# A 4096x4096x4096 matrix product with leaky ReLU: regions that fill PSUM, A transposed once by VectorE in 32x32 blocks with a permuted k, B streamed, order fixed by hand

## The chip, the core and the metric

One core of a Trainium2 chip. The metric is the device time of one launch in microseconds (us). The executions of the kernel before agree within about 0.3%. The profile is one execution, its span 1 to 2 us below the timed one.

## The reference

```python
# a: 4096 x 4096, b: 4096 x 4096, float32; alpha = 0.01
x = np.matmul(a, b)
return np.where(x > 0, x, alpha * x)
```

## The kernel before

It multiplies in bf16. For each of four blocks of 1024 columns it loads B as 32 tiles of 128x1024 and casts them into one cache; then it goes through the 32 row tiles of A. In the first block A is cast, stored as bf16 in DRAM, and transposed by TensorE; in the other three it comes back through a transposing DMA.

```python
b_3d = b.rearrange("(ko ki) n -> ki ko n", ki=P)
...
b_cache_pool = ctx.enter_context(tc.tile_pool(name="b_cache", bufs=1))
b_load_pool = ctx.enter_context(tc.tile_pool(name="b_load", bufs=3))
...
for nb in range(N_BLOCKS):
    b_cache = b_cache_pool.tile([P, K_TILES, N_BLOCK], BF16)
    for ko in range(K_TILES):
        b_ld = b_load_pool.tile([P, N_BLOCK], FP32)
        nc.sync.dma_start(b_ld, b_3d[:, ko, nb * N_BLOCK:(nb + 1) * N_BLOCK])
        nc.any.tensor_copy(b_cache[:, ko, :], b_ld)
    for mo in range(M_TILES):
        aT = at_pool.tile([P, K_TILES, P], BF16)
        if nb == 0:
            # ... load t_in, cast to t_bf, store t_bf to DRAM ...
            for ko in range(K_TILES):
                tp = at_psum_pool.tile([P, P], BF16)
                nc.tensor.transpose(tp, t_bf[:, ko * P:(ko + 1) * P], ident)
                nc.vector.tensor_copy(aT[:, ko, :], tp)
        else:
            nc.sync.dma_start_transpose(aT, a_bf_dram[mo][:])
        for nt in range(NT_PER_BLOCK):
            # ... 32 matmuls 128x512 into one PSUM bank, Lrelu on ScalarE, store ...
```

Of the kernel before, what the change touches and what calls it, by code (L numbers as in the profile page):

```python
# [1 line left out]

# [5 lines left out]


@with_exitstack
def kernel(
    ctx: ExitStack,
    tc: tile.TileContext,
    a: bass.AP,
    b: bass.AP,
    alpha,
    out: bass.AP,
):
    nc = tc.nc  # L20
    P = 128
    M, K = a.shape
    K2, N = b.shape
    assert K == K2
    BF16 = mybir.dt.bfloat16
    FP32 = mybir.dt.float32

    M_TILES = M // P
    K_TILES = K // P
    N_TILE = 512  # L30
    N_BLOCK = 1024
    N_BLOCKS = N // N_BLOCK
    NT_PER_BLOCK = N_BLOCK // N_TILE

    alpha = float(alpha)

    a_3d = a.rearrange("(mo mi) k -> mi mo k", mi=P)
    b_3d = b.rearrange("(ko ki) n -> ki ko n", ki=P)
    out_3d = out.rearrange("(mo mi) n -> mi mo n", mi=P)

    dram_pool = ctx.enter_context(tc.tile_pool(name="dram", bufs=M_TILES, space=bass.MemoryType.DRAM))
    a_bf_dram = [dram_pool.tile([P, K], BF16, name=f"a_bf_{i}") for i in range(M_TILES)]

    ident_pool = ctx.enter_context(tc.tile_pool(name="ident", bufs=1))
    ident = ident_pool.tile([P, P], BF16)
    make_identity(nc, ident)

    a_ld_pool = ctx.enter_context(tc.tile_pool(name="a_ld", bufs=2))
    a_bf_pool = ctx.enter_context(tc.tile_pool(name="a_bfp", bufs=2))
    at_pool = ctx.enter_context(tc.tile_pool(name="at", bufs=3))  # L50
    at_psum_pool = ctx.enter_context(tc.tile_pool(name="at_psum", bufs=2, space=bass.MemoryType.PSUM))

    b_cache_pool = ctx.enter_context(tc.tile_pool(name="b_cache", bufs=1))
    b_load_pool = ctx.enter_context(tc.tile_pool(name="b_load", bufs=3))

    psum_pool = ctx.enter_context(tc.tile_pool(name="psum", bufs=4, space=bass.MemoryType.PSUM))
    o_pool = ctx.enter_context(tc.tile_pool(name="oo", bufs=4))

    for nb in range(N_BLOCKS):
        b_cache = b_cache_pool.tile([P, K_TILES, N_BLOCK], BF16)  # L60
        for ko in range(K_TILES):
            b_ld = b_load_pool.tile([P, N_BLOCK], FP32)
            nc.sync.dma_start(b_ld, b_3d[:, ko, nb * N_BLOCK:(nb + 1) * N_BLOCK])  # L63
            nc.any.tensor_copy(b_cache[:, ko, :], b_ld)  # L64

        for mo in range(M_TILES):
            aT = at_pool.tile([P, K_TILES, P], BF16)
            if nb == 0:
                t_in = a_ld_pool.tile([P, K], FP32)
                nc.sync.dma_start(t_in, a_3d[:, mo, :])  # L70
                t_bf = a_bf_pool.tile([P, K], BF16)
                nc.any.tensor_copy(t_bf, t_in)  # L72
                nc.sync.dma_start(a_bf_dram[mo][:], t_bf)  # L73
                for ko in range(K_TILES):
                    tp = at_psum_pool.tile([P, P], BF16)
                    nc.tensor.transpose(tp, t_bf[:, ko * P:(ko + 1) * P], ident)  # L76
                    nc.vector.tensor_copy(aT[:, ko, :], tp)  # L77
            else:
                nc.sync.dma_start_transpose(aT, a_bf_dram[mo][:])  # L79

            for nt in range(NT_PER_BLOCK):
                psum = psum_pool.tile([P, N_TILE], FP32)
                for ko in range(K_TILES):
                    nc.tensor.matmul(  # L84
                        psum,
                        aT[:, ko, :],
                        b_cache[:, ko, nt * N_TILE:(nt + 1) * N_TILE],
                        start=(ko == 0),
                        stop=(ko == K_TILES - 1),
                    )  # L90
                o_sb = o_pool.tile([P, N_TILE], FP32)
                nc.scalar.activation(  # L92
                    o_sb, psum, mybir.ActivationFunctionType.Lrelu, alpha=alpha
                )
                nc.sync.dma_start(  # L95
                    out_3d[:, mo, nb * N_BLOCK + nt * N_TILE: nb * N_BLOCK + (nt + 1) * N_TILE],
                    o_sb,
                )


# [1 line left out]
_INS = ['a', 'b', 'alpha']  # L102
_OUTS = [((4096, 4096), 'float32')]
#: Inputs that are plain numbers.
_NUMBERS = {'alpha': 0.009999999776482582}


# [26 lines left out]
```

## Time and profile before

| | |
|---|---|
| time | 2023.7 us (2021.2 to 2024.8) |
| matmul pace in quiet stretches | 215.8 ns |
| bytes moved, mean rate | 337 MB, 167 GB/s |
| granted TensorE clock, mean | 0.974 |

In a line of the groups, the part after the first bar is the busy time and the mean of one instruction, and the part after the second is how long the engine sat idle just before such instructions, with what ended the wait. In a table of stretches the last three numbers are the granted clock, the mean busy share of the 16 DMA engines and GB/s. The prediction below shows the lines and reads them.

### The profile page before, as it was taken

To read this page: it belongs to the slowest core of one execution; us is meant where nothing else is said; L and a number is where in the kernel's file an instruction comes from. 1 tells how busy PE (TensorE), PEld (TensorE's weight loads), DVE (VectorE), ACT (ScalarE), POOL (GpSimd) and SP (SyncE) were. 2 spreads that over 40 slices of the span, in tenths; PEclk is the share of its full clock that TensorE was granted. 3 is DMA by queue.
4 is the path that set the end of the run, shared out by engine and by line. 5 is a ranking of instruction groups with operands and counts; after the bars stand their busy time and mean duration, and the time that the engine had idled before them with its cause. 6 is when DMAs were issued, how large, how long until landed. Compare 5 with 4: busy or idle time off the path is not lost.

```text
span 2022.0 us, 21113 instructions
## 1 busy us (share of the span) xinstructions
PE 1870.9 (93%) x9032; PEld 865.5 (43%) x9216; DVE 232.5 (11%) x1033; ACT 390.8 (19%) x409; POOL 0.7 (0%) x6
## 2 busy tenths in 40 slices
PE   4699999999977999999995999999997799999999
PEld 1244445555432444444442344444443244444444
DVE  1244444444410000000000000000000000000000
ACT  5423222222224000000015100000002400000000
POOL 0000000000000000000000000000000000000000
PEclk8799999999999999999998999999998999999999
DMA  8975666665379554554558754554556855554552
GB/s 302 344 289 219 229 233 237 237 231 219 141 214 264 125 112 107 125 105 114 125 108 280 194 120 101 123 109 111 124 117 185 246 126 106 116 121 107 116 120 63
DMA packets 460894, 336.95 MB, mean 167 GB/s; under 512 B 403456, under 2 KB 403456, under 8 KB 452608
## 3 DMA queue, kind: packets, MB, share of 16 engines
q1 hardware_dynamic: 460800, 335.59, 60.2%
q8 instruction: 72, 1.18, 0.2%
q14 instruction: 22, 0.18, 0.0%
HBM read 134.22 MB, written 100.66 MB: 116 GB/s over the span
## 4 chain that ended last, share of the span: by engine, by line
PE 85%; DMA 10%; ACT 2%; SPq 1%; DVE 1%; issue 1%; ACTq 0%
PE psum L84 82%; DMA b_ld<-in_b_dram 9%; PE tp L76 3%; ACT b_cache L64 2%; DVE aT L77 1%; SPq L79 1%; DMA t_in<-in_a_dram 1%; ACT t_bf L72 0%; SPq L63 0%; SPq L95 0%; DVE b_cache L64 0%; SPq L73 0%; ACT o_sb L92 0%; ACTq L92 0%
## 5 line engine op out<-in xcount | busy, mean ns | idle before, releaser
L84 PE MATMUL psum<-b_cache,aT 128*128 128x512 bf16 x8008 | 1859.0, 383 | 111.1 <-ACT b_cache L64 100.4
L84 PEld LDWEIGHTS <-aT 128*128 128x128 bf16 x8192 | 804.2, 99 | 1115.4 <-issue 179.6
L92 ACT ACTIVATE o_sb<-psum 128x512 f32<-128x512 f32 x256 | 151.6, 596 | 1274.0 <-PE psum L84 1121.9
L77 DVE COPY aT<-tp 128x128 bf16<-128x128 bf16 x1024 | 226.5, 224 | 327.0 <-PE tp L76 284.6
L76 PE MATMUL tp<-ident,t_bf 128*128 128x128 bf16 x1024 | 219.3, 221 | 36.4 <-ACT t_bf L72 25.7
L72 ACT CAST t_bf<-t_in 128x4096 bf16<-128x4096 f32 x32 | 115.4, 3606 | 231.3 <-PE tp L76 220.0
L64 ACT CAST b_cache<-b_ld 128x1024 bf16<-128x1024 f32 x119 | 124.3, 1044 | 122.4 <-DMA b_ld<-in_b_dram 122.4
L64 DVE CAST b_cache<-b_ld 128x1024 bf16<-128x1024 f32 x9 | 6.0, 692 | 979.7 <-PE psum L84 966.3
L76 PEld LDWEIGHTS <-t_bf 128*128 128x128 bf16 x1024 | 99.7, 99 | 37.1 <-ACT t_bf L72 26.5
L64 ACT ACT_TABLE_LOAD x1 | 1.3, 1283 | 0.7 <-PEq L115 0.7
L92 ACT ACT_TABLE_LOAD x1 | 1.3, 1283 | 0.0
masks.py:199 POOL TENSOR_SCALAR_AFFINE_SELECT ident<-ident 128x128 bf16<-128x128 bf16 x1 | 0.3, 294 | 0.1
masks.py:197 POOL MEMSET ident<- 128x128 bf16 x1 | 0.2, 205 | 0.3 <-POOLq L115 0.3
L115 POOL MEMSET const-bfloat16-1.0<- 128x1 bf16 x1 | 0.1, 102 | 0.0
L115 POOL MEMSET const-uint8-127<- 128x1 uint8 x1 | 0.1, 102 | 0.0
L115 POOL MEMSET const-float32-0.0<- 128x1 f32 x1 | 0.1, 99 | 0.2 <-issue 0.2
L115 POOL MEMSET const-float32-1.0<- 128x1 f32 x1 | 0.1, 99 | 0.0
## 6 DMA issues: line engine op xcount, KB each, us to landing
b_ld<-in_b_dram SPq DMA_DIRECT2D x128, 512.0 KB, 4.5
t_in<-in_a_dram SPq DMA_DIRECT2D x32, 2048.0 KB, 10.1
out_dram<-o_sb SPq DMA_DIRECT2D x256, 256.0 KB, 2.5
a_bf<-t_bf SPq DMA_DIRECT2D x32, 1024.0 KB, 4.1
aT<-a_bf SPq DMA_TRANSPOSE x96, 7.3
```

The lines of the kernel that those rows point to most:

```text
L64: nc.any.tensor_copy(b_cache[:, ko, :], b_ld)
L72: nc.any.tensor_copy(t_bf, t_in)
L76: nc.tensor.transpose(tp, t_bf[:, ko * P:(ko + 1) * P], ident)
L77: nc.vector.tensor_copy(aT[:, ko, :], tp)
L79: nc.sync.dma_start_transpose(aT, a_bf_dram[mo][:])
L84: nc.tensor.matmul(psum, aT[:, ko, :], b_cache[:, ko, nt * N_TILE:(nt + 1) * N_TILE], start=(ko == 0), stop=(ko == K_TILES - 1),)
L92: nc.scalar.activation(o_sb, psum, mybir.ActivationFunctionType.Lrelu, alpha=alpha)
L115: nc = _bacc.Bacc("TRN2", target_bir_lowering=False, num_devices=1)
```

## The change

The intent: keep TensorE at its pace all the time. A region of 512x1024 outputs takes the eight PSUM buffers of the kernel, 128x512 each. The contraction is cut into four units of 1024. A strip is 1024 columns of B (32 tiles, 16.8 MB), and two regions use it, one after the other. B's tiles are loaded ahead into five buffers instead of one block with a stop. A is transposed once, by VectorE, in blocks of 32x32: so a row group of 32 partitions gets another quarter of the unit's k (`q`), and B's rows have to come in the same permuted order. Nine matmuls on zeros stand at the start (L131 in the profiles). The diff is shortened; dots and brackets mark what is left out, and `mm` is one matmul.

```diff
+    a_v = a.rearrange("(mt g i) (u q w) -> mt u q i g w", g=4, i=32, q=4, w=QW)
+    b_v = b.rearrange("(u q c j) n -> u c q j n", u=KU, q=4, c=KC, j=32)
+    at_pool = ctx.enter_context(tc.tile_pool(name="at", bufs=HALVES * KU + 2))
+    bt_pool = ctx.enter_context(tc.tile_pool(name="bt", bufs=KU + 1))
+    a32_pool = ...bufs=4   a16_pool = ...bufs=2   b32_pool = ...bufs=4
+    psum_pool = ...bufs=8
+    ctx.enter_context(tc.manual_schedule())
+    def load_a(mb, h, u, mt):
+        tile_no = (mb * HALVES + h) * MT + mt
+        a32 = a32_pool.tile([P, 4, QW], FP32, name="a32")
+        for g in range(4):
+            nc.sync.dma_start(a32[:, g, :], a_v[tile_no, u, :, :, g, :])
+        a16 = a16_pool.tile([P, 4, QW], BF16, name="a16")
+        nc.vector.tensor_copy(a16, a32)
+        dst = at[mb, h, u][:, :, mt * P:(mt + 1) * P].rearrange("p c (g i) -> p g c i", g=4)
+        nc.vector.transpose(dst, a16.rearrange("p g (c j) -> p g c j", c=KC))
+    def load_b(pair, n, u, c):
+        b32 = b32_pool.tile([P, RN], FP32, name="b32")
+        nc.sync.dma_start(b32, b_v[u, c, :, :, n * RN:(n + 1) * RN])
+        nc.scalar.copy(bt[pair, u][:, c, :], b32)
 ... (the order: two row regions per strip of B, strips in snake order, the next strip's
 ...  loads and casts put into the second region's four steps, A's next rows nine steps ahead)
+            for mt in range(MT):
+                for c in range(KC):
+                    for nt in range(NP):
+                        mm(banks[mt, nt], mb, h, pi, u, mt, nt, c)
+                if u == KU - 1:
+                    for nt in range(NP):
+                        o = o_pool.tile([P, NT], FP32, name="o")
+                        nc.scalar.activation(o, banks[mt, nt], Lrelu, alpha=alpha)
+                        nc.scalar.dma_start(out[row:row + P, col:col + NT], o)
-    (the B block with its refill, the bf16 copy of A, both kinds of transposes)
```

More of the change, by code (lines that the diff above doesn't have):

```diff
@@ L5 @@
 import concourse.tile as tile
-from concourse import bass_utils, mybir
+from concourse import mybir
 from concourse._compat import with_exitstack
-from concourse.masks import make_identity
+P = 128
+BF16 = mybir.dt.bfloat16
+FP32 = mybir.dt.float32
+KC = 8
+NT = 512
+MT = 4
+NP = 2
 @with_exitstack
@@ L20 @@
     nc = tc.nc
-    P = 128
     M, K = a.shape
@@ L24 @@
     assert K == K2
-    BF16 = mybir.dt.bfloat16
-    FP32 = mybir.dt.float32
-    M_TILES = M // P
-    K_TILES = K // P
-    N_TILE = 512
-    N_BLOCK = 1024
-    N_BLOCKS = N // N_BLOCK
-    NT_PER_BLOCK = N_BLOCK // N_TILE
-    alpha = float(alpha)
-    a_3d = a.rearrange("(mo mi) k -> mi mo k", mi=P)
-    b_3d = b.rearrange("(ko ki) n -> ki ko n", ki=P)
-    out_3d = out.rearrange("(mo mi) n -> mi mo n", mi=P)
-    dram_pool = ctx.enter_context(tc.tile_pool(name="dram", bufs=M_TILES, space=bass.MemoryType.DRAM))
@@ L42 @@
-    a_bf_dram = [dram_pool.tile([P, K], BF16, name=f"a_bf_{i}") for i in range(M_TILES)]
-    ident_pool = ctx.enter_context(tc.tile_pool(name="ident", bufs=1))
-    ident = ident_pool.tile([P, P], BF16)
-    make_identity(nc, ident)
-    a_ld_pool = ctx.enter_context(tc.tile_pool(name="a_ld", bufs=2))
-    a_bf_pool = ctx.enter_context(tc.tile_pool(name="a_bfp", bufs=2))
-    at_pool = ctx.enter_context(tc.tile_pool(name="at", bufs=3))
-    at_psum_pool = ctx.enter_context(tc.tile_pool(name="at_psum", bufs=2, space=bass.MemoryType.PSUM))
@@ L53 @@
-    b_cache_pool = ctx.enter_context(tc.tile_pool(name="b_cache", bufs=1))
-    b_load_pool = ctx.enter_context(tc.tile_pool(name="b_load", bufs=3))
-    psum_pool = ctx.enter_context(tc.tile_pool(name="psum", bufs=4, space=bass.MemoryType.PSUM))
-    o_pool = ctx.enter_context(tc.tile_pool(name="oo", bufs=4))
-    for nb in range(N_BLOCKS):
-        b_cache = b_cache_pool.tile([P, K_TILES, N_BLOCK], BF16)
-        for ko in range(K_TILES):
-            b_ld = b_load_pool.tile([P, N_BLOCK], FP32)
-            nc.sync.dma_start(b_ld, b_3d[:, ko, nb * N_BLOCK:(nb + 1) * N_BLOCK])
-            nc.any.tensor_copy(b_cache[:, ko, :], b_ld)
-        for mo in range(M_TILES):
-            aT = at_pool.tile([P, K_TILES, P], BF16)
-            if nb == 0:
-                t_in = a_ld_pool.tile([P, K], FP32)
-                nc.sync.dma_start(t_in, a_3d[:, mo, :])
-                t_bf = a_bf_pool.tile([P, K], BF16)
-                nc.any.tensor_copy(t_bf, t_in)
-                nc.sync.dma_start(a_bf_dram[mo][:], t_bf)
-                for ko in range(K_TILES):
-                    tp = at_psum_pool.tile([P, P], BF16)
-                    nc.tensor.transpose(tp, t_bf[:, ko * P:(ko + 1) * P], ident)
-                    nc.vector.tensor_copy(aT[:, ko, :], tp)
-            else:
-                nc.sync.dma_start_transpose(aT, a_bf_dram[mo][:])
-            for nt in range(NT_PER_BLOCK):
-                psum = psum_pool.tile([P, N_TILE], FP32)
-                for ko in range(K_TILES):
-                    nc.tensor.matmul(
-                        psum,
-                        aT[:, ko, :],
-                        b_cache[:, ko, nt * N_TILE:(nt + 1) * N_TILE],
-                        start=(ko == 0),
-                        stop=(ko == K_TILES - 1),
-                    )
-                o_sb = o_pool.tile([P, N_TILE], FP32)
-                nc.scalar.activation(
-                    o_sb, psum, mybir.ActivationFunctionType.Lrelu, alpha=alpha
-                )
-                nc.sync.dma_start(
-                    out_3d[:, mo, nb * N_BLOCK + nt * N_TILE: nb * N_BLOCK + (nt + 1) * N_TILE],
-                    o_sb,
-                )
@@ new lines @@
+    alpha = float(alpha)
+    KU = K // (KC * P)
+    RM = MT * P
+    RN = NP * NT
+    HALVES = 2
+    MB = M // (HALVES * RM)
+    NB = N // RN
+    QW = KC * P // 4
+    a_v = a.rearrange("(mt g i) (u q w) -> mt u q i g w", g=4, i=32, q=4, w=QW)
+    b_v = b.rearrange("(u q c j) n -> u c q j n", u=KU, q=4, c=KC, j=32)
+    at_pool = ctx.enter_context(tc.tile_pool(name="at", bufs=HALVES * KU + 2))
+    bt_pool = ctx.enter_context(tc.tile_pool(name="bt", bufs=KU + 1))
+    a32_pool = ctx.enter_context(tc.tile_pool(name="a32", bufs=4))
@@ new lines, with new_a @@
+    a16_pool = ctx.enter_context(tc.tile_pool(name="a16", bufs=2))
+    b32_pool = ctx.enter_context(tc.tile_pool(name="b32", bufs=4))
+    o_pool = ctx.enter_context(tc.tile_pool(name="oo", bufs=4))
+    warm_pool = ctx.enter_context(tc.tile_pool(name="warm", bufs=1))
+    psum_pool = ctx.enter_context(tc.tile_pool(name="psum", bufs=8, space=bass.MemoryType.PSUM))
+    ctx.enter_context(tc.manual_schedule())
+    at = {}
+    bt = {}
+    def new_a(mb, h, u):
+        at[mb, h, u] = at_pool.tile([P, KC, RM], BF16, name="at")
@@ new lines, in new_b @@
+    def new_b(pair, n, u):
+        bt[pair, u] = bt_pool.tile([P, KC, RN], BF16, name="bt")
+    def load_b(pair, n, u, c):
+        b32 = b32_pool.tile([P, RN], FP32, name="b32")
+        nc.sync.dma_start(b32, b_v[u, c, :, :, n * RN:(n + 1) * RN])
+        nc.scalar.copy(bt[pair, u][:, c, :], b32)
+    regions = []
+    pairs = []
+    for mb in range(MB):
+        order = list(range(NB)) if mb % 2 == 0 else list(range(NB - 1, -1, -1))
+        for n in order:
+            if not pairs or pairs[-1] != n:
+                pairs.append(n)
+            for h in range(HALVES):
+                regions.append((mb, h, len(pairs) - 1, n))
@@ new lines @@
+    jobs = {}
+    for s_region, (mb, h, pi, n) in enumerate(regions):
+        if h:
+            continue
+        for u in range(KU):
+            if regions[s_region - 1][2] != pi or s_region == 0:
+                s = s_region * KU + u
+                jobs.setdefault(max(0, s - KU), []).append(("b", pi, n, u, s))
+            if s_region and regions[s_region - 1][0] != mb:
+                for hh in range(HALVES):
+                    idx = hh * KU + u
+                    s = s_region * KU + idx
+                    jobs.setdefault(s - HALVES * KU - 1, []).append(("a", mb, hh, u, s))
@@ new lines, with run @@
+    jobs = {s: [j for j in v if not (j[0] == "b" and j[1] == 0)] for s, v in jobs.items()}
+    def run(job):
+        if job[0] == "a":
+            _, mb, h, u, _ = job
+            new_a(mb, h, u)
+            for mt in range(MT):
+                load_a(mb, h, u, mt)
+        else:
+            _, pi, n, u, _ = job
+            new_b(pi, n, u)
+            for c in range(KC):
+                load_b(pi, n, u, c)
+    w = warm_pool.tile([P, NT], BF16, name="w")
+    nc.vector.memset(w, 0.0)
@@ new lines, with first_unit @@
+    wp = psum_pool.tile([P, NT], FP32, name="ps")
+    for i in range(9):
+        nc.tensor.matmul(wp, w[:, :P], w, start=True, stop=True)
+    def first_unit(u):
+        new_a(0, 0, u)
+        new_b(0, 0, u)
+        for what in "ababbabbabbb":
+            if what == "a":
+                load_a(0, 0, u, first_unit.a)
+                first_unit.a += 1
+            else:
+                load_b(0, 0, u, first_unit.b)
+                first_unit.b += 1
+        first_unit.a = first_unit.b = 0
@@ new lines, with mm @@
+    first_unit.a = first_unit.b = 0
+    def mm(ps, mb, h, pi, u, mt, nt, c):
+        nc.tensor.matmul(
+            ps,
+            at[mb, h, u][:, c, mt * P:(mt + 1) * P],
+            bt[pi, u][:, c, nt * NT:(nt + 1) * NT],
+            start=(u == 0 and c == 0),
+            stop=(u == KU - 1 and c == KC - 1),
+        )
+    first_unit(0)
+    for r, (mb, h, pi, n) in enumerate(regions):
+        banks = {}
+        for u in range(KU):
+            s = r * KU + u
+            if r == 0:
+                if u + 1 < KU:
+                    first_unit(u + 1)
+                else:
+                    for uu in range(KU):
+                        new_a(0, 1, uu)
+                        for mt in range(MT):
+                            load_a(0, 1, uu, mt)
+            for job in jobs.get(s, []):
+                run(job)
+            if u == 0:
+                for mt in range(MT):
+                    for nt in range(NP):
+                        banks[mt, nt] = psum_pool.tile([P, NT], FP32, name="ps")
+            if r == 0 and u < KU - 1:
+                na = nb = 0
+                for what in "ababbabbabbb":
+                    if what == "a":
+                        todo = [(na, c) for c in range(nb)]
+                        na += 1
+                    else:
+                        todo = [(mt, nb) for mt in range(na)]
+                        nb += 1
+                    for mt, c in todo:
+                        for nt in range(NP):
+                            mm(banks[mt, nt], mb, h, pi, u, mt, nt, c)
+                continue
+            for mt in range(MT):
+                for c in range(KC):
+                    for nt in range(NP):
+                        mm(banks[mt, nt], mb, h, pi, u, mt, nt, c)
+                if u == KU - 1:
+                    for nt in range(NP):
+                        o = o_pool.tile([P, NT], FP32, name="o")
+                        nc.scalar.activation(
+                            o, banks[mt, nt], mybir.ActivationFunctionType.Lrelu, alpha=alpha
+                        )
+                        row = ((mb * HALVES + h) * MT + mt) * P
+                        col = n * RN + nt * NT
+                        nc.scalar.dma_start(out[row:row + P, col:col + NT], o)
```

## The prediction

> **What bounds the kernel now.** I read the page first, then the timeline of its last microseconds, then tables of stretches, then the chain of waits inside one refill. The page first:
>
> ```profile
> span 2022.0 us, 21113 instructions
> ...
> PE 1870.9 (93%) x9032; PEld 865.5 (43%) x9216; DVE 232.5 (11%) x1033; ACT 390.8 (19%) x409; POOL 0.7 (0%) x6
> ...
> L76 PE MATMUL tp<-ident,t_bf 128*128 128x128 bf16 x1024 | 219.3, 221 | 36.4 <-ACT t_bf L72 25.7
> ...
> L64 ACT CAST b_cache<-b_ld 128x1024 bf16<-128x1024 f32 x119 | 124.3, 1044 | 122.4 <-DMA b_ld<-in_b_dram 122.4
> ```
>
> TensorE is the bound, but 93% busy isn't 93% of its best, since the records overlap (383 ns mean against the pace below). The true pace comes from the evictions in the timeline of the end, one per accumulation of 32 matmuls:
>
> ```profile
> 2004.75 0.60 ACT L92 ACTIVATE o_sb<-psum 128x512 f32<-128x512 f32 x1 [6.31 <-PE psum L84]
> ...
> 2011.65 0.60 ACT L92 ACTIVATE o_sb<-psum 128x512 f32<-128x512 f32 x1 [6.31 <-PE psum L84]
> 2018.56 0.60 ACT L92 ACTIVATE o_sb<-psum 128x512 f32<-128x512 f32 x1 [6.31 <-PE psum L84]
> ```
>
> They are 6.905 us apart: 215.8 ns a matmul. Both kernels need 4096*4096*4096 / (128*128*512) = 8192 of them, so the floor is 8192 x 0.2158 = 1767.8 us, and 254 us of the span are over it. Where? The stretches (time, PE, PEld, DVE, ACT, POOL, granted clock, DMA share, GB/s):
>
> ```profile
> 30.00:40.00 10.00, 5.13 (x12) 1.39 (x12) 0.00 (x0) 5.22 (x5) 0.00 (x0) 0.59 0.85 278
> ...
> 60.00:70.00 10.00, 3.88 (x8) 0.77 (x6) 0.00 (x0) 5.50 (x6) 0.00 (x0) 0.50 1.02 388
> ...
> 580.00:600.00 20.00, 9.53 (x31) 3.38 (x31) 0.00 (x0) 8.36 (x8) 0.00 (x0) 0.83 0.95 297
> 600.00:620.00 20.00, 11.94 (x42) 4.30 (x42) 0.00 (x0) 11.48 (x11) 0.00 (x0) 0.91 0.87 283
> ...
> 1200.00:1300.00 100.00, 99.47 (x455) 45.30 (x463) 0.00 (x0) 8.45 (x15) 0.00 (x0) 1.00 0.53 116
> ```
>
> In the quiet stretch 100 us hold 463 weight loads, one per matmul, at clock 1.00. From 580 to 640 the stretches hold about a third of that. The chain of waits names it (start, length, what):
>
> ```profile
> 599.48 4.42 DMA b_ld<-in_b_dram
> 603.91 0.02 issue
> 603.93 1.05 ACT b_cache L64
> 604.98 0.02 issue
> 605.00 4.44 DMA b_ld<-in_b_dram
> ```
>
> The B block has one buffer: its successor is loaded only after the last matmul on it, through three staging tiles, each cycle 4.4 us of transfer and 1.05 us of cast, so 1.83 us a tile and about 58 us for 32 tiles.
>
> The 254 us split like this. The first block's last matmul ends at 576.4 us; the other three need 3 x 2048 x 0.2158 = 1325.8 us, and the last matmul ends near 2018.5, so the three refills cost 116 us. Before 576.4, 134 us are lost: from 80 to 576 us there are 1978 matmul weight loads (426.9 us) and 980 for transposes, so 69 us, some 70 ns each, go to transposes; the first 80 us hold the other 70 matmuls (15 us), so 65 us are the start. The tail is 3.5 us.
>
> **What the Trainium skill says.** "TensorE: Matmul & The Clock Gate", section "Wait — 56ns, not 53.3ns?", gives 215.7 ns from start to start for 512 columns once warm; the trace agrees (215.8), so there is nothing to gain inside the steady state. "Perfetto Trace Analysis", section "Identifying the Most-Contended Engine", warns that matmul busy time is not closeness to the roofline; 93% busy against 1768/2022 = 87% agrees. "DMA: Bandwidth & Descriptors", section "Measured (HBM→SBUF, 128 partitions, SWDGE, issued from GpSimd)", lists 341 GB/s at 1 MB and 425 at 16 MB for one transfer; here the trace shows 278 to 297 with three 512 KB tiles in turn and 388 with a 2 MB load beside them. "VectorE: DVE Perf Modes", section "The three transpose paths", has VectorE transposing only within 32x32 blocks, 311 ns for 128x128 bf16; no run shows it yet.
>
> **The change, part by part.**
>
> *Removed:* all 1024 TensorE transposes and their PSUM copies (69 us), the bf16 copy of A in DRAM with its 96 transposing DMAs (off the path), and the single-buffered B block with its three stops (116 us).
>
> *Regions.* 512x1024 outputs fill all eight banks; a region is 256 matmuls, 55.24 us, in four k units of 64 matmuls (13.8 us); 32 regions. An eviction takes 0.60 us. A bank is wanted again when the next region reaches it, so evictions are hidden if ScalarE is free.
>
> *A by VectorE.* 128 tiles, each a cast 128x1024 (0.69 us, the VectorE row of the same shape in the group list by form) and a block transpose. Estimate from the skill's 311 ns and the 0.96 GHz that the same page lists for this engine, at one column a cycle: 896 more columns add 0.93, so 1.25 us. Four tiles make 7.8 us a unit, under 13.8: hidden.
>
> *B streamed.* 13 loads of a 4096x1024 strip (the snake order saves three of 16), 416 casts x 1.044 = 434 us on ScalarE, plus 256 x 0.6 = 154: a third of the span. But a strip is loaded during one region only: 16.8 MB in 55 us is 304 GB/s. With five B buffers, the casts of a unit wait until the unit before it in that region is done, and four staging tiles may land ahead. At 1.45 us a tile (three cycles of 5.45 us overlapped gave 1.83, four give 1.37 if the transfer keeps up), the eight casts of the last unit end some 10 us into its 13.8 us. ScalarE works in order and has the region's evictions behind those casts, so they begin then, and the first bank is ready about 2 us before it is wanted. So no stall, with a small margin.
>
> *Start.* The first region needs 8.4 MB of A and 16.8 MB of B. I take 340 GB/s, between the 283 with three tiles in turn and the 388 with more in flight: the build shows eight DMA completion counters shared by all transfers, and A comes in pieces of 128 KB with 1 KB rows, so I stay below 388. 2.5 + 25.2/0.340 = 76.5 us. TensorE keeps up, except that the last unit runs row tile by row tile, and about 50 of its matmuls wait for its last B tile: 1.05 (cast) + 50 x 0.2158 + 2 (some at the half clock that the start of the trace shows, 0.50) = 13.9. Region 0 ends at 90.4; loss 35 us, against 65 now.
>
> *Second and third region.* The loads go on with the other 8.4 MB of A (25 us, plus some 2 us because output transfers share the counters), and only then B's second strip (49 us): 76.5 + 27 + 49.4 = 153. Region 1 would end at 145.6, but its evictions stand behind the strip's last cast: 153 + 1.05 + 1.2 = 155.3. **Loss 10 us**, once.
>
> *Sum.* 155.3 + 30 x 55.24 = 1812.5; two last evictions and the last output transfer 4.5 (2.5 landing in the list of DMA issues): span 1817. The timed median is 1.9 us above the profiled span of before: 1819. I round to 1818.
>
> **The rivals.**
> - *B can't keep pace.* At today's 283 GB/s, 28 tiles take 51 us after four early ones, and with cast and eviction the region ends 2 to 4 us late, 12 times: 1845 to 1865. For it: 278 to 297 GB/s in today's refills. Against: there the cycle was set by three buffers, with the DMA engines 0.85 busy.
> - *VectorE becomes the bound.* If the scattered output slows the block transpose to 4 us, four tiles need 19 us a unit; some 100 us more over three changes of A: about 1920. For it: no row of today's trace has this instruction. Against: the estimate leaves a factor of almost two.
> - *The start is free of the bandwidth limit.* At 400 GB/s the first region's data are there at 65 us and the later stall is gone: about 1798. The trace held 433 GB/s only for 5 us.
> - *Half clock.* If the first region's gaps keep the clock at 0.50, its tail doubles: 11 us more.
>
> **Range and chances.** Total time moves with the first 50.3 MB: at 300 GB/s it is about 1838, at 380 about 1803. A small stall at some strip changes would add up to 20. So 1798 to 1845, and the tail is longer above. Even the VectorE rival stays faster by 5%, so faster 0.97.
>
> **What would show it.** Right: pace still 55.24 us a region from the third on; matmul weight loads 463 per 100 us; clock 1.00; no transposes on TensorE; the longest TensorE waits on ScalarE casts in the first 90 us, and one gap near 146 to 155 us that waits for evictions; DMA near 340 GB/s until 150 us. Wrong: gaps at every second region's start (B too slow), TensorE waiting for VectorE (transpose slow), a pace above 216 ns, or DMA far from 340 at the start.

## The result

The changed kernel takes **3525.6 us** (3524.1 to 3529.2), against 2023.7 us before: ratio 1.743, interval 1.741 to 1.746. A ratio here is the mean time of one kernel's fast runs over that of the other's in the same rounds, so not quite the ratio of the medians.

The page of the changed kernel: span, busy times, slices of DMA share, the chain of waits by line, and three groups.

```profile
span 3522.3 us, 19708 instructions
...
PE 1895.5 (54%) x8201; PEld 824.1 (23%) x8201; DVE 248.5 (7%) x257; ACT 585.5 (17%) x674; POOL 0.2 (0%) x4
...
DMA  2223231222323222222233222222233222122221
...
DMA b<-in_b_dram 55%; SPq L72 18%; PE ps L148 18%; ACT bt L84 4%; DMA a<-in_a_dram 3%; ACT o L196 1%; SPq L83 0%; ACTq L201 0%; DVE a L74 0%; ACTq L196 0%; DVEq L74 0%
...
L148 PE MATMUL ps<-bt,at 128*128 128x512 bf16 x8192 | 1891.5, 394 | 1621.3 <-ACT o L196 1442.5
...
L84 ACT CAST bt<-b 128x1024 bf16<-128x1024 f32 x416 | 431.3, 1044 | 1640.9 <-DMA b<-in_b_dram 1636.3
...
L76 DVE STREAM_TRANSPOSE at<-a 128x1024 bf16<-128x1024 bf16 x128 | 159.4, 1245 | 5.9
```

TensorE now sits idle for 1621 us, and the group line puts 1443 of it down to ScalarE's evictions. That is only the last link: ScalarE itself waits 1636 us for B's tiles, and the chain that sets the end is 55% B transfers. Yet the DMA engines are 0.2 to 0.3 busy in almost every slice. A queue that everything waits for, on engines that are three quarters idle, is what the reader should stop at. The 18% of `SPq L72` in the chain is the queue issuing A's loads: 1.28 us each by the median for 128 KB, so about 103 GB/s, the same rate again.

The stretches of the changed kernel, one inside a load of a strip and one in the region after it:

```profile
594.00:712.00 118.00, 32.52 (x151) 14.67 (x150) 0.00 (x0) 24.02 (x23) 0.00 (x0) 0.66 0.26 105
738.00:783.00 45.00, 45.00 (x204) 20.15 (x203) 0.00 (x0) 3.58 (x6) 0.00 (x0) 0.97 0.12 45
```

While B is loaded, the rate is 105 GB/s at a share of 0.26, and 0.26 x 16 is about four engines. The timeline of the end of that load shows the cadence, and what TensorE waited for:

```profile
702.53 1.04 ACT L84 CAST bt<-b 128x1024 bf16<-128x1024 f32 x1 [3.95 <-DMA b<-in_b_dram]
...
707.52 1.04 ACT L84 CAST bt<-b 128x1024 bf16<-128x1024 f32 x1 [3.95 <-DMA b<-in_b_dram]
...
718.46 0.59 ACT L196 ACTIVATE o<-ps 128x512 f32<-128x512 f32 x1
...
719.10 0.58 PE L148 MATMUL ps<-bt,at 128*128 128x512 bf16 x1 [92.58 <-ACT o L196]
```

A B tile arrives every 4.99 us, not every 1.45. A strip of 32 takes 160 us, and only after its last cast does ScalarE reach the finished region's evictions: TensorE had waited 92.6 us for the first.

### The profile page after: what moved, and what is told of

It reads as the page before. It is cut to its first block, busy times and chain, and to the rows that moved or that the text cites. A ratio compares the mean times of both kernels' runs of the same rounds, so it can differ in the third digit from the quotient of the medians.

```text
span 3522.3 us, 19708 instructions
## 1 busy us (share of the span) xinstructions
PE 1895.5 (54%) x8201; PEld 824.1 (23%) x8201; DVE 248.5 (7%) x257; ACT 585.5 (17%) x674; POOL 0.2 (0%) x4
## 3 DMA queue, kind: packets, MB, share of 16 engines
q8 instruction: 64, 1.05, 0.1%
## 4 chain that ended last, share of the span: by engine, by line
DMA 58%; SPq 18%; PE 18%; ACT 4%; issue 1%; ACTq 0%; DVE 0%; DVEq 0%
DMA b<-in_b_dram 55%; SPq L72 18%; PE ps L148 18%; ACT bt L84 4%; DMA a<-in_a_dram 3%; ACT o L196 1%; SPq L83 0%; ACTq L201 0%; DVE a L74 0%; ACTq L196 0%; DVEq L74 0%
## 5 line engine op out<-in xcount | busy, mean ns | idle before, releaser
L148 PE MATMUL ps<-bt,at 128*128 128x512 bf16 x8192 | 1891.5, 394 | 1621.3 <-ACT o L196 1442.5
L148 PEld LDWEIGHTS <-at 128*128 128x128 bf16 x8192 | 823.0, 101 | 2690.2 <-issue 1709.2
L84 ACT CAST bt<-b 128x1024 bf16<-128x1024 f32 x416 | 431.3, 1044 | 1640.9 <-DMA b<-in_b_dram 1636.3
L196 ACT ACTIVATE o<-ps 128x512 f32<-128x512 f32 x256 | 152.8, 597 | 1292.3 <-PE ps L148 771.0
L74 DVE CAST a<-a 128x1024 bf16<-128x1024 f32 x128 | 88.8, 694 | 2510.0 <-DMA a<-in_a_dram 2491.6
L76 DVE STREAM_TRANSPOSE at<-a 128x1024 bf16<-128x1024 bf16 x128 | 159.4, 1245 | 5.9
L131 PE MATMUL ps<-w 128*128 128x512 bf16 x9 | 4.0, 628 | 1.2 <-DVE w L128 1.2
L131 PEld LDWEIGHTS <-w 128*128 128x128 bf16 x9 | 1.2, 139 | 3.1 <-issue 2.0
```

Of the source, the lines that this page charges most:

```text
L74: nc.vector.tensor_copy(a16, a32)
L76: nc.vector.transpose(dst, a16.rearrange("p g (c j) -> p g c j", c=KC))
L84: nc.scalar.copy(bt[pair, u][:, c, :], b32)
L131: nc.tensor.matmul(wp, w[:, :P], w, start=True, stop=True)
L148: nc.tensor.matmul(ps, at[mb, h, u][:, c, mt * P:(mt + 1) * P], bt[pi, u][:, c, nt * NT:(nt + 1) * NT], start=(u == 0 and c == 0), stop=(u ...
L196: nc.scalar.activation(o, banks[mt, nt], mybir.ActivationFunctionType.Lrelu, alpha=alpha)
```

## The experiments

**The theories.** *Engine count:* "DMA: Bandwidth & Descriptors", section "Why a DMA increments its semaphore by 16 and not by 1", says that a transfer is spread over the largest number of engines up to 16 that divides the slowest dimension of both its patterns, and that the lowest-numbered ones are taken. In the changed kernel both loads have the quarter `q` as slowest dimension, count 4. *Order:* the evictions stand behind casts on ScalarE, and this costs whatever the rate is. *Counters:* the traces show eight completion counters (semaphores that a transfer raises when it lands), which loads and outputs share, so a load may have to wait for an output, and the reverse; the load queue waited 624 us for outputs. Twelve kernels were run, all correct. Runs with a single execution are given by that execution, with state unknown.

**1. Both loads cut by quarter**, so that the slowest dimension is 32 rows.

```diff
-        for g in range(4):
-            nc.sync.dma_start(a32[:, g, :], a_v[tile_no, u, :, :, g, :])
+        for q in range(4):
+            nc.sync.dma_start(a32[32 * q:32 * (q + 1), :, :], a_v[tile_no, u, q])
-        nc.sync.dma_start(b32, b_v[u, c, :, :, n * RN:(n + 1) * RN])
+        for q in range(4):
+            nc.sync.dma_start(b32[32 * q:32 * (q + 1), :], b_v[u, c, q, :, n * RN:(n + 1) * RN])
```

> Both loads are cut by quarter of the k unit, so the slowest dimension of every load is 32 rows instead of 4 quarters; bytes, tiles, orders and instructions of the engines stay, only the B loads become four times as many. Theory 1 (a load whose slowest dimension is 4 runs on 4 of 16 engines): loads go from 105 GB/s to some 300 or more, DMA share at the start from 0.26 to over 0.8, time near 1820 to 1850 us. Theory 2 (ScalarE has the evictions behind the casts, whatever the transfer rate): waits of TensorE for evictions stay several hundred us and the time stays above 2500. Theory 3 (eight completion counters shared by loads and outputs block the loads): four times as many B transfers share the same counters, so the time doesn't fall, or rises above 3500.

Measured: 2120.6 us (2116.6 to 2124.0), ratio to before 1.048. The 1400 us come from the shape of the transfers alone, for bytes, tiles and orders are as they were; B's transfers are also four times as many and a quarter of the size; number 3 tests whether more pieces help by themselves. But the stretch of this run below shows 243 GB/s with the engines at 1.00, not 340: the theory's number for this form was too good by 270 us.

```profile
160.00:225.00 65.00, 17.61 (x82) 7.90 (x81) 0.00 (x0) 31.46 (x31) 0.00 (x0) 0.67 1.00 243
```

**2. One stride for B.** A is cut as above; B stays whole, but k is permuted so that partition p holds row 8p + c.

```diff
-    b_v = b.rearrange("(u q c j) n -> u c q j n", u=KU, q=4, c=KC, j=32)
+    b_v = b.rearrange("(u p c) n -> u c p n", u=KU, c=KC, p=P)
-        nc.sync.dma_start(b32, b_v[u, c, :, :, n * RN:(n + 1) * RN])
+        nc.sync.dma_start(b32, b_v[u, c, :, n * RN:(n + 1) * RN])
-        nc.vector.transpose(dst, a16.rearrange("p g (c j) -> p g c j", c=KC))
+        nc.vector.transpose(dst, a16.rearrange("p g (j c) -> p g c j", c=KC))
```

> Same as the split of A, but B isn't cut: the k permutation is changed so that a B tile's 128 rows have one stride (partition p has row 8p+c), and the block transpose reads A with a step of 8 elements. B stays 416 transfers of 512 KB. Theory 1: 16 engines again, time at or a little below that of the split of both, 1800 to 1835 us, unless the stepped read slows the block transpose above 3 us (then VectorE shows it). Theories 2 and 3: above 2500 us, since neither the order nor the counters change.

Measured: 1889.3 us (1885.0 to 1897.5), ratio 0.933, so faster than before. The stretch is that of B's second strip; the chain's line is what follows it.

```profile
160.00:195.00 35.00, 4.04 (x19) 1.75 (x18) 0.00 (x0) 22.98 (x22) 0.00 (x0) 0.61 0.95 337
```

```profile
197.68 388.46 PE ps L148 x1790
```

B comes at 337 GB/s, and once TensorE starts the third region at 197.7 us it is the bound for 388 us on end: seven regions of 256 matmuls at 215.8 ns are 386.7. The expectation was still missed by 54 us: the start is slower than I took it (below), and TensorE later waited seven more times for evictions, 22 us in all. The stepped read costs VectorE 2.01 us a transpose against 1.245.

**3. Each B tile as two halves**, 64 partitions each, slowest dimension 2, A as delivered. This parts the exact rule from "more pieces run in parallel".

```diff
-        nc.sync.dma_start(b32, b_v[u, c, :, :, n * RN:(n + 1) * RN])
+        for q in range(0, 4, 2):
+            nc.sync.dma_start(b32[32 * q:32 * (q + 2), :], b_v[u, c, q:q + 2, :, n * RN:(n + 1) * RN])
```

> The changed kernel with each B tile loaded by two transfers of two quarters (64 partitions, slowest dimension 2); A as it was. Theory 1 in its exact form (engine count is the largest divisor up to 16 of the slowest dimensions, lowest-numbered engines): both halves use the same 2 engines, B comes at some 52 GB/s, 10 us a tile, and the time rises to 5500 to 6200 us. If cutting a transfer only adds parallel work: same as 3525 us or faster. Theory 3: a few per cent slower.

Measured: 5455 us, just under the stated span. A stretch inside a strip's load:

```profile
1000.00:1100.00 100.00, 0.00 (x0) 0.00 (x0) 0.00 (x0) 10.44 (x10) 0.00 (x0) 0.50 0.13 53
```

0.13 x 16 is two engines, at 53 GB/s. Two transfers in flight did not give four engines: both ran on the same two. Per engine it is 26 GB/s, as with four.

The traces also hold the count itself, though no view prints it: the updates that landing transfers make to the completion counters. In the kernel before, in number 1 and in number 2 they come to 16 for each transfer. With 16 for each output, the delivered kernel has 5 for each load (8736 updates are 928 x 5 + 256 x 16), and this run has 3 for each half of a B tile (9152 are 512 x 5 + 832 x 3 + 256 x 16). That fits four and two engines with one update more. What fell is the number of engines; each was no slower, 26 GB/s against 21 in number 2 (337/16).

**4. The kernel before with 4-quarter loads of B**, nothing else of the change (the cast of A writes the permuted order, so the result is right).

```diff
-    b_3d = b.rearrange("(ko ki) n -> ki ko n", ki=P)
+    b_3d = b.rearrange("(q ko j) n -> ko q j n", q=4, j=32)
-            nc.sync.dma_start(b_ld, b_3d[:, ko, nb * N_BLOCK:(nb + 1) * N_BLOCK])
+            nc.sync.dma_start(b_ld, b_3d[ko, :, :, nb * N_BLOCK:(nb + 1) * N_BLOCK])
-                nc.any.tensor_copy(t_bf, t_in)
+                nc.any.tensor_copy(
+                    t_bf.rearrange("p (ko q j) -> p ko q j", q=4, j=32),
+                    t_in.rearrange("p (q ko j) -> p ko q j", q=4, j=32),
+                )
```

> The kernel before, with one thing of the change: k is permuted so that each B tile is read as 4 quarters of 32 rows, slowest dimension 4; the cast of A writes the permuted order, so the result stays right. Bytes, tile sizes, number of transfers, buffers and schedule stay. Engine-count theory: a B tile goes from 1.83 to 5.0 us, a refill of 32 tiles from 58 to 160 us, four times 100 us more: 2350 to 2480 us, and DMA near 105 GB/s with a share near 0.25 in the refills. If the slow loads of the changed kernel came from its schedule or its shared counters, this one stays at 2024 to 2050.

Measured: 2421 us. A stretch in the load of its second B block, the first of the three refills:

```profile
700.00:760.00 60.00, 20.82 (x45) 6.14 (x45) 0.00 (x0) 12.53 (x12) 0.00 (x0) 0.50 0.26 105
```

The same 105 GB/s at 0.26, with the old schedule and the old buffers. So neither is needed for the slow loads.

**5 and 6. One load at a time.** Number 5 is number 2 with A's loads as delivered; number 6 is the delivered kernel with A cut by quarter.

> B with one row stride (16 engines), A still in 4-quarter pieces. A alone then comes at 105 GB/s: 160 us for the 16.8 MB of a change of A, which has 110 us of regions to hide in, so some 50 us lost three times, and some 100 us more at the start (16.8 MB of A at 105 GB/s against the 140 us they took, B in between). Engine-count theory: 2050 to 2250 us. If only B's rate matters: 1890 as with both.

> The changed kernel with only A cut by quarter (16 engines); B stays in 4-quarter transfers. Engine-count theory: B's 218 MB at 105 GB/s are 13 strips of 160 us, with about 50 us of a region after each in which nothing is loaded: some 13 x 213 = 2770, and A's phases shrink to the 110 us of their two regions, 3 x 110: 3050 to 3250 us. If A's 128 KB pieces were the main trouble: below 2500.

Measured: 2172 us with only B mended, 3275 with only A (25 us over what was stated). From 3526 us, B's shape alone is worth 1354 us and A's alone 251; both, in the form of number 2, 1636 (numbers 5 and 6 are single executions). B has 218 MB in 13 strips, A 67 MB.

**7. Casts of B on VectorE, loads as delivered.**

```diff
-        nc.scalar.copy(bt[pair, u][:, c, :], b32)
+        nc.vector.tensor_copy(bt[pair, u][:, c, :], b32)
```

> The changed kernel with its 4-quarter loads, but the casts of B go to VectorE, so ScalarE has only evictions. Theory 1: load rate stays 105 GB/s (5.0 us a B tile), and the 285 MB of loads alone take 2720 us, so the time falls to some 2750 to 3000 us at best and not further. Theory 2: the waits for evictions (1443 us) go and the time comes near 2100 us or below.

Measured: 3239 us: 286 us gained, not the 525 to 775 that I had allowed at best. The waits of this run say why: evictions no longer stand behind casts, but ScalarE also issues the outputs, and an output waits for a counter that a slow B load holds.

```profile
ACT o L196 <- DMA b<-in_b_dram: 1212.4, 103, 70.6
PE ps L148 <- ACT o L196: 1047.1, 103, 54.9
```

**8. Outputs issued by GpSimd, loads as delivered.** These transfers have counters of their own: in the trace they raise eight others than the loads do.

```diff
-                        nc.scalar.dma_start(out[row:row + P, col:col + NT], o)
+                        nc.gpsimd.dma_start(out[row:row + P, col:col + NT], o)
```

> The changed kernel, only the outputs are issued by GpSimd with completion counters of their own, so that no load waits for an output (624 us of such waits of the load queue in the changed kernel). Theory 3 (shared counters are the cause): most of the 1500 us comes back, below 2600. Engine-count theory: the loads are just as slow, and what is gained is at most the prefetch of four tiles, 15 to 20 us a strip: 3250 to 3500 us.

Measured: 3329 us, 197 us gained. The load queue's 624 us of waits for outputs are gone. ScalarE no longer issues the outputs either, so the gain is that of both.

**9. Both of these, loads as delivered.**

> The changed kernel with its 4-quarter loads, B's casts on VectorE and the outputs issued by GpSimd with counters of their own: neither casts nor counters can hold an eviction any more. Engine-count theory: the load queue never pauses for long, so the time comes near the 285 MB at 105 GB/s, 2720 us, plus the last two regions, 2750 to 2950, and never below 2720. If order and counters were the larger part of the loss: below 2400.

Measured: 3010 us, 60 over the stated span: 516 us gained of the 1636 that the pattern gives. (It ran on another chip, where the kernel before took 2019.6 us.) In its profile TensorE waits for no eviction any more; it waits 876 us for the casts of B's tiles as they land. Order and counters are real costs on top of slow loads, but with 285 MB at 105 GB/s no order can go below some 2720 us, and none did.

**10. One stride, and casts on VectorE** (number 2 with the edit of number 7).

> The one-stride version (1889 us), with B's casts on VectorE, so ScalarE's evictions no longer stand behind them. Order theory for the remaining loss: region 2 then starts at some 157 us, when its first B unit is there, instead of 198, and ends near 210 instead of 253; the short waits for evictions later (22 us) go as well: 1820 to 1850 us. If the start is bound by the bytes alone: 1880 to 1890.

Measured: 1841.0 us (1837.0 to 1844.2), ratio 0.909. Moving the casts gave 48 us at full rate; TensorE's waits for evictions, 55 us in number 2, are gone.

**11. The same, and outputs issued by GpSimd.**

> The previous one, and the outputs issued by GpSimd, whose transfers have completion counters of their own, so that no load waits for an output. If the shared counters cost something by now (740 us of waits of the load queue for outputs in the one-stride version, most of them harmless): 10 to 25 us faster than the previous one, 1800 to 1830. If harmless: within 5 us of it, or slower where GpSimd issues its transfers more slowly.

Measured: **1830.5 us** (1828.6 to 1837.5), ratio 0.905 (0.902 to 0.908), against 0.909 (0.908 to 0.911) for number 10, the intervals just touching, so a gain over number 10 isn't shown. This is the lowest time of all. All the waits of TensorE in its profile:

```profile
PE ps L148 <- DVE bt L84: 19.8, 10, 4.6
PE ps L148 <- DVE at L76: 16.4, 7, 3.4
PE ps L131 <- DVE w L128: 1.2, 1, 1.2
```

They are all in the first 200 us; a query of the waits after that returns none.

**12. B cut into four by columns** (number 2, but four transfers of 128 partitions in rows of 1 KB). It asks why number 1 had only 243 GB/s. "SBUF — State Buffer", section "Door 1: The DMA port swizzle (why `[64,N]` ≈ `[32,N]`)", says that bandwidth depends on how many of the 16 ports the partitions reach; by its table 32 neighbouring partitions reach eight.

```diff
-        nc.sync.dma_start(b32, b_v[u, c, :, n * RN:(n + 1) * RN])
+        for w4 in range(4):
+            cw = RN // 4
+            nc.sync.dma_start(b32[:, w4 * cw:(w4 + 1) * cw], b_v[u, c, :, n * RN + w4 * cw:n * RN + (w4 + 1) * cw])
```

> The one-stride version (1889 us), each B tile cut into four transfers of 128 KB, but by columns: each has all 128 partitions in rows of 1 KB. It has the same number and size of transfers as the version that cuts by quarter (2120 us, 240 GB/s at a DMA share of 1.0), which has 32 partitions in rows of 4 KB. If what holds that one is that 32 partitions reach only half of the ports into SBUF: B here at 300 GB/s or more and 1880 to 1950 us. If it is the number of transfers or the eight counters: 240 GB/s and 2080 to 2150 us again.

Measured: 2045 us, between the two stated spans. In its second strip:

```profile
165.00:215.00 50.00, 7.06 (x33) 3.13 (x32) 0.00 (x0) 27.13 (x27) 0.00 (x0) 0.62 0.91 272
```

272 GB/s at 0.91, where number 1 had 243 at 1.00 and whole tiles 337 at 0.95. Inconclusive: with all ports in reach it is a little faster, but most of the distance to whole tiles stays. The load queue needs 0.43 us for each of the four issues in this run's chain, so 1.72 us a tile by itself, and the rows are four times shorter. It also reads B in the order of number 2, with rows 128 KB apart and not 16. How much each of these costs stays open.

## Why the prediction was wrong

It said 1818 us, and faster with a chance of 0.97.

- **The step that failed is the transfer rate**, in two places of the working: under *B streamed*, "At 1.45 us a tile (three cycles of 5.45 us overlapped gave 1.83, four give 1.37 if the transfer keeps up)", and under *Start*, "I take 340 GB/s, between the 283 with three tiles in turn and the 388 with more in flight". The number was carried over from transfers whose slowest dimension is 128 to transfers whose slowest dimension is 4. It measured 105 GB/s and 4.99 us a tile; the prediction's own sign of being wrong, DMA far from 340 at the start, came with 98 GB/s in the first 100 us. Number 4 shows the same from the old kernel; number 3 shows that the count follows the dimension. The page that holds the rule was open; I read its bandwidth tables and not the count of engines, and asked how large the pieces are, not over how many engines they go.
- **The rival "B can't keep pace" was named and bounded wrongly.** It took today's 278 to 297 GB/s as the lower end and made 1845 to 1865 of it. It treated bandwidth as a limit that the chip sets for all kernels, not as one that a pattern can cut.
- **The order was seen, its price was not.** The prediction has "ScalarE works in order and has the region's evictions behind those casts", and called it a small margin. With tiles every 5 us it became waits of 93 and 156 us. At full rate moving the casts was worth 48 us (number 10), not the single 10 us.
- **Right: the pace.** With 16 engines TensorE ran regions at 215.8 ns a matmul, and from 200 us on nothing held it in number 11.
- **Right: VectorE.** The block transpose takes 1.245 us (estimated 1.25), four tiles of A 7.8 us a unit; the rival of a slow transpose did not come.
- **Right in kind, off in size: start and second strip.** With whole tiles the third region began at 197.7 us, not at 155.3: the first 80 us ran at some 277 GB/s (about 300 from 20 to 60 us at a DMA share of 1.05), and the stepped transpose kept VectorE 19.8 of 20 us busy from 120 to 140 us. With casts and counters moved as well, 1830.5 us comes near 1818, but in part by luck: its first region ended at 111.1 us, not at 90.4, and the 10 us of the second were not lost. It is also another kernel; the forecast of the delivered one stays wrong.
- **Slips that change nothing:** from 580 to 640 us the stretches hold 115 weight loads where the quiet pace gives 278, so two fifths and not a third; and the sum is 1819, not 1818.

## What to carry to other kernels

Before a load's pattern is changed, look at its slowest dimension, not only at its bytes and row length: a view that splits the partitions into 4 x 32 brought the same bytes at under a third of the rate here (105 against 337 GB/s), and a different permutation (8p + c instead of q, c, j) kept one stride. When a profile shows everything waiting for DMA and a DMA share near 4/16 or 2/16, count engines before touching buffers or order. On an engine that works in order, keep what frees PSUM ahead of, or away from, work that waits for transfers.

## What the Trainium skill lacked or had wrong

- "DMA: Bandwidth & Descriptors": the rule for the number of engines stands in the section on semaphore increments and in a row of its closing rules for kernel authors, but neither there, nor in its bandwidth section, nor in the DMA advice of "Perfetto Trace Analysis" is a measured rate: 105 GB/s at a slowest dimension of 4 and 53 at 2, against 337 for tiles of the same size at 128. The number of engines came out as the rule has it at each of these.
- The same page gives about 27 GiB/s an engine (29 GB/s); the runs show 26 GB/s with rows of 4 KB (105/4, 53/2).
- The same page says that issuing from several engines only saves issue time. Issuing the outputs from GpSimd was worth 197 us here with slow loads (at full rate the 10 us are not clear of the noise). It gave the outputs completion counters of their own and took their issue, with its waits, from ScalarE; the two were not parted. No page has what sharing the counters costs.
- "SBUF — State Buffer": it has figures for one transfer to 32 partitions and for two in flight, but none for transfers to all four groups of 32 partitions in turn: 243 GB/s here, with the cause not parted from the number of transfers and their issue time.
- "VectorE: DVE Perf Modes" gives the block transpose at 128x128 only, 311 ns. At 128x1024 it took 1245 ns, and 2011 ns when its input was read with a step of 8 bf16 elements; no page has a figure for the latter.
